# One core's log-sum-exp over 16384 rows: the first 8.4 MB load issued as four loads of growing size

## The chip, the cores and the metric

The kernel runs on one core of one Trainium2 chip. The metric is the time of one execution on the device in microseconds (us), as the median of repeated runs; less is better. A profile of one execution, taken by the hardware profiler, stands beside the times. In it the engines are called ACT (the scalar engine, which does the exponentials), DVE (the vector engine, which does the sums), POOL (the third elementwise engine, which takes part of the sums), PE (the matrix engine, hardly used here) and SP (the engine that issues the transfers). "SPq" is SP's instruction queue.

## The reference

```python
def reference(x):                      # x: float32 [32, 512, 1024]
    max_x = np.max(x, axis=-1, keepdims=True)
    return max_x.squeeze(-1) + np.log(np.sum(np.exp(x - max_x), axis=-1))
```

There are 32 x 512 = 16384 rows of 1024 numbers, 67.1 MB in all, and each gives one number. The inputs are drawn from a standard normal distribution.

## The kernel before, in words

**Rows and partitions.** The 16384 rows are dealt over 128 partitions, 128 rows to each. The first 112 rows of a partition (W) lie next to one another in the input, so that a load of s rows is, for each partition, one stretch of s x 4 KB; neighbouring partitions are 112 x 4 KB = 448 KB apart. The last 16 rows of each partition (B) come from a second region of the input, in which partitions are 64 KB apart.

**Without the maximum.** The kernel takes exp(x) directly, sums it and takes the logarithm. Beside this it keeps a check that no sum has left a range in which that is accurate; only if the check fails does it read everything again and compute the reference's form (L312 to L361). In the profiled execution it does not fail, and this part is a skipped branch at the end.

**Loads and their work.** The table `LOADS` (L23) lists 18 loads by their size in rows of a partition: four of 16 rows (8.4 MB each), then 13.5, 12.5, 9, 7, 6, 4.47 and so on down to 0.53 and 0.47 rows. Beside each size stands what is done with its rows: "R16" is one Exp on ACT over everything (L228) and one summing instruction on DVE (L239); "F" lets POOL first add the two halves of each row (L233), and DVE sums what is left (L171); "T" sums row by row on DVE (L249); the last row comes as "Y" and "Z", in which ACT sums while it takes the Exp (L202).

**The ring.** Data lands in `ring`, 48 rows of each partition. The loads go round it. All of them are issued by SP, in order, by `load` (L134 to L141): ahead of a load that would overwrite rows still in use, SP waits for the DVE or ACT instruction that read them last. The first three loads fill the empty ring and wait for nothing; the fourth waits until DVE has summed the rows of the first.

**What ACT waits for.** Each load has a semaphore of its own, `landed[i]`, which rises by 16 when the whole load has landed. ACT waits for that value before the first Exp on a load (`act.wait(landed[i], 16)` in the loop over the loads, L186 on).

**The opening.** A program begins with barriers in which all engines wait for one another, and only after these come the kernel's instructions: the load of ACT's table (L125), four small DVE memsets (L126 to L129), and SP's loads. The hook `start_early` (L378) moves one instruction: after the program has been built, it takes the first load out of its place and puts it in SP's stream ahead of SP's first DRAIN, which is SP's part in the first barrier. So the first load is issued as the very first instruction, and the second load only after the barriers.

**The end.** While the last loads land, ACT takes the logarithm of the first 112 columns (L268) and SP stores them (L276); the last 16 columns follow (L279, L281, L285), with the check's last steps beside them on DVE and PE (L290 to L308).

Of the kernel before, what the change touches and what calls it, by code (L numbers as in the profile page):

```python
# [15 lines left out]
RING = 48  # L16
B = 16
LATE = 119

# [31 lines left out]
def kernel(  # L53
# [5 lines left out]
    nc = tc.nc  # L59
# [24 lines left out]
    def source(e0, size):  # L84
        assert e0 >= W * d or e0 + size <= W * d
        return x_rest[:, e0 - W * d : e0 - W * d + size] if e0 >= W * d else x_rows[:, e0 : e0 + size]
# [8 lines left out]
    def sbuf(name, cols, dtype=fp32, rows=P):  # L95
        return nc.alloc_sbuf_tensor(name, [rows, cols], dtype).ap()

    ring = sbuf("ring", RING * d)
# [15 lines left out]
    landed = [nc.alloc_semaphore(f"landed{i}") for i in range(len(loads))]  # L114
    act = Counted(nc, nc.scalar, "act")
# [18 lines left out]
    def load(i, here, done_before, size):  # L134
        for a, b, who, at in users:
            if a < here + size and b > here:
                sp.wait(who, at)
        users[:] = [u for u in users if not (u[0] < here + size and u[1] > here)]
        return nc.sync.dma_start(
            out=ring[:, here : here + size], in_=source(done_before, size)  # L140
        ).then_inc(landed[i], 16)  # L141

    def check_early():
        dve.wait(act, summed_by_act)
        dve.wait(dve, dve.n)
        dve.did(nc.vector.tensor_scalar(  # L146
            out=clamped[:, 0:LATE], in0=sumexp[:, 0:LATE],
            scalar1=LOW, scalar2=HIGH, op0=ALU.max, op1=ALU.min,
        ))
        dve.wait(dve, dve.n)  # L150
        dve.did(nc.vector.scalar_tensor_tensor(  # L151
            out=clamped[:, 0:LATE], in0=clamped[:, 0:LATE], scalar=0.0, in1=sumexp[:, 0:LATE],
            op0=ALU.bypass, op1=ALU.not_equal, accum_out=bad[:, 0:1],
# [4 lines left out]
    def add_up(c, who, **kw):  # L158
        pe.wait(*who)
        return pe.did(nc.tensor.matmul(count, lhsT=ones, rhs=sumexp[:, c : c + 1], **kw))  # L160
# [3 lines left out]
    def reduce_folded():  # L164

        nonlocal early_sum
        while folded:
            c0, s0, p0, n0 = folded.pop(0)
            halves = ring[:, p0 : p0 + s0 * d].rearrange("p (c d) -> p c d", d=d)[:, :, 0:H]
            dve.wait(pool, n0)  # L170
            at = dve.did(nc.vector.reduce_sum(  # L171
                out=sumexp[:, c0 : c0 + s0], in_=halves, axis=AX.X
            ))
            users.append((p0, p0 + s0 * d, dve, at))
            if c0 < W:
                early_sum = at
# [3 lines left out]
    here = 0  # L180
    early_sum = 0
    done_before = 0
    summed_by_act = 0
    ln_early = None
    first_load = None
    for i, (size, ops) in enumerate(loads):  # L186
        if here + size > RING * d:
            assert here == p
            p = here = 0
        if any(q < here + size and q + t * d > here for _, t, q, _ in folded):  # L190
            reduce_folded()
        dma = load(i, here, done_before, size)
        first_load = first_load or dma.ins
        end = here + size
        done_before += size
        act.wait(landed[i], 16)
        for k, (how, s) in enumerate(ops):
            rows = ring[:, p : p + s * d].rearrange("p (c d) -> p c d", d=d)
            if how in "YZ":

                assert c == LAST and (how == "Z" or here == p)
                at = act.did(nc.scalar.activation(  # L202
                    out=last_exp[:, here - p : end - p], in_=ring[:, here:end], func=AF.Exp,
                    accum_out=first_sum if how == "Y" else last_sum,
                ))
                if how == "Z":
                    last_piece = ring[:, here:end]
                here = end
                if how == "Y":
                    nc.vector.addr_align(128, offset=0, max_nops=0)  # L210
                    dve.wait(act, at)
                    first_piece = dve.did(nc.vector.tensor_copy(out=sumexp[:, LAST:NC], in_=first_sum))  # L212
                summed_by_act = at
            elif how == "A":
                assert here == p
                v = ring[:, p : p + d]
                at = act.did(nc.scalar.activation(
                    out=v, in_=v, func=AF.Exp, accum_out=sumexp[:, c : c + 1]
                ))
                here += d  # L220
                users.append((p, p + d, act, at))
                summed_by_act = at
                who = (act, at)
            else:

                upto = end if k + 1 == len(ops) and c + s < LAST else p + s * d
                v = ring[:, here:upto]
                at = act.did(nc.scalar.activation(out=v, in_=v, func=AF.Exp))  # L228
                here = upto
            if how == "F":  # L230
                reduce_folded()
                pool.wait(act, at)
                at = pool.did(nc.gpsimd.tensor_tensor(  # L233
                    out=rows[:, :, 0:H], in0=rows[:, :, 0:H], in1=rows[:, :, H:d], op=ALU.add
                ))
                folded.append((c, s, p, at))
            elif how == "R":
                dve.wait(act, at)
                who = (dve, dve.did(nc.vector.reduce_sum(  # L239
                    out=sumexp[:, c : c + s], in_=rows, axis=AX.X  # L240
                )))
                users.append((p, p + s * d, *who))
            elif how == "T":
                if c >= W:
                    reduce_folded()
                dve.wait(act, at)
                for r in range(s):
                    lo = rows[:, r, 0:H]
                    who = (dve, dve.did(nc.vector.scalar_tensor_tensor(  # L249
                        out=lo, in0=lo, scalar=1.0, in1=rows[:, r, H:d],  # L250
                        op0=ALU.mult, op1=ALU.add, accum_out=sumexp[:, c + r : c + r + 1],
                    )))
                    users.append((p + r * d, p + (r + 1) * d, *who))
                    if c + r >= LATE:
                        add_up(c + r, who, start=False, stop=False)
            if how == "A" and c >= LATE:
                add_up(c, who, start=False, stop=False)
            if how in "RT":
                if c < W:
                    early_sum = dve.n  # L260
                reduce_folded()
            c += s
            p += s * d
            if c == LATE:

                act.wait(dve, early_sum)
                act.wait(act, early_act)
                ln_early = act.did(nc.scalar.activation(  # L268
                    out=res[:, 0:W], in_=sumexp[:, 0:W], func=AF.Ln
                ))  # L270
                check_early()
            if c <= W:
                early_act = summed_by_act
        assert here == end
# [7 lines left out]
        out=res[:, LAST:NC], in_=last_sum, func=AF.Ln, bias=sumexp[:, LAST:NC]  # L282
# [7 lines left out]
    dve.did(nc.vector.scalar_tensor_tensor(  # L290
        out=clamped[:, LATE:NC], in0=sumexp[:, LATE:NC], scalar=LOW,
        in1=sumexp[:, LATE:NC], op0=ALU.max, op1=ALU.not_equal, accum_out=bad[:, 1:2],
# [9 lines left out]
        out=over[:, 0:half], in0=last_piece[:, 0:half], scalar=CEILING,  # L302
# [16 lines left out]
    with nc.If(all_fine < 1):  # L319
# [5 lines left out]
        for c0 in range(0, NC, RING):  # L325
# [6 lines left out]
            for c1, c2 in ((c0, edge), (edge, c0 + s)):  # L332
                if c1 == c2:
                    continue
                nc.scalar.dma_start(
                    out=ring[:, (c1 - c0) * d : (c2 - c0) * d],
                    in_=source(c1 * d, (c2 - c1) * d),
# [4 lines left out]
                out=neg, in_=v, op=ALU.max, axis=AX.X, negate=True  # L342
# [3 lines left out]
                out=v, in0=v, in1=neg[:, :, None].to_broadcast([P, s, d])  # L346
# [5 lines left out]
                out=sumexp[:, c0 : c0 + s], in_=v, axis=AX.X  # L352
# [25 lines left out]
    def start_early(program):  # L378

        blocks = program.main_func.blocks  # L380
        here = next(b for b in blocks if any(i.name == first_load.name for i in b.instructions))
        k = next(k for k, i in enumerate(here.instructions) if i.name == first_load.name)
        assert not here.instructions[k].has_wait()
        first = here.instructions.pop(k)
        top = blocks[0].instructions
        k = next(
            k for k, i in enumerate(top)
            if i.engine == mybir.EngineType.SP and isinstance(i, mybir.InstDrain)
        )
        top.insert(k, first)  # L390

    nc.at_finalize(start_early)


# [28 lines left out]
```

## Time and profile before

| what | value |
|---|---|
| time before, median of 3 runs | 161.67 us (161.58 to 161.69) |
| profiled execution: span from its first to its last instruction | 160.4 us |
| what the median has beyond that span | 1.3 us |
| first Exp on ACT starts | 22.00 us after the first instruction |
| second Exp starts | 41.33 us |
| last instruction ends | 160.4 us |

The first instruction of the span is the issue of the first load, and its start is the zero of all times of the trace. No time of its own is listed for the profiled execution apart from its span; the part of a run that lies outside the span is taken from the median, 161.67 - 160.4 = 1.3 us. In the trace an idle stretch of an engine is shown in brackets ahead of the instruction that ended it, with what it had waited for. The lists of transfers count packets in the window in which they start; a load is 128 packets of data, one for each partition, and 16 tiny ones (one for each of the core's 16 DMA engines) that report its end, which gives the page's count: 18 loads and 2 stores of 144 packets are 2880.

### The profile page before, as it was taken

The page shows a single profiled execution, that of the slowest core. Times are in us where ns is not written, and L with a number is a line of the kernel's source. Part 1 is how long each engine was busy: PE and PEld are TensorE (multiplying, and loading weights), DVE is VectorE, ACT ScalarE, POOL GpSimd, SP SyncE. Part 2 cuts the span into 40 slices and gives each one's busy share as a digit, 9 for nine tenths or more (in the row PEclk, how much of TensorE's full clock was granted, in tenths as well). Part 3 has the DMA queues.
Part 4 walks back from the last instruction along what each step waited for, and adds up shares of the span by engine and source line. Part 5 has one row for each costly group of instructions (what it writes and reads, how often), then busy time and mean ns, then how long its engine had stood idle before and what let it go on. Part 6 is the DMA issues. An engine that isn't in the chain of part 4 may idle for free.

```text
span 160.4 us, 219 instructions
## 1 busy us (share of the span) xinstructions
PE 2.2 (1%) x26; PEld 1.1 (1%) x26; DVE 114.3 (71%) x59; ACT 114.5 (71%) x31; POOL 37.3 (23%) x11
## 2 busy tenths in 40 slices
PE   0000000000000000000000000000000000000022
PEld 0000000000000000000000000000000000000011
DVE  0000000009999499994999859959999999999996
ACT  3000059990699708995099949991999989799996
POOL 0000000000000000000000994690004969891000
DMA  7996996996996996996999999999999999999992
GB/s 262 523 523 262 523 523 262 523 507 278 523 490 294 523 490 294 523 490 294 482 441 441 441 425 409 409 409 480 432 395 417 450 416 398 448 411 424 412 413 95
DMA packets 2881, 67.18 MB, mean 419 GB/s; under 512 B 576, under 2 KB 704, under 8 KB 1344
## 3 DMA queue, kind: packets, MB, share of 16 engines
q1 hardware_dynamic: 2880, 67.18, 97.7%
q14 instruction: 1, 0.01, 0.0%
HBM read 67.11 MB, written 0.07 MB: 419 GB/s over the span
## 4 chain that ended last, share of the span: by engine, by line
DMA 52%; ACT 28%; DVE 19%; issue 1%; PE 0%
DMA ring<-in_x_dram 52%; ACT ring L228 27%; DVE sumexp L239 15%; DVE sumexp L171 2%; DVE ring L249 1%; DVE over L301 0%; PE count L306 0%; ACT res L268 0%; DVE clamped L290 0%; DVE fine L308 0%; DVE sumexp L212 0%
## 5 line engine op out<-in xcount | busy, mean ns | idle before, releaser
L228 ACT ACTIVATE ring<-ring 128x16384 f32<-128x16384 f32 (+16 forms) x23 | 111.7, 4908 | 43.0 <-DMA ring<-in_x_dram 43.0
L239 DVE TENSOR_REDUCE sumexp<-ring 128x16 f32<-128x16384 f32 (+4 forms) x9 | 85.6, 9513 | 42.7 <-ACT ring L228 42.7
L233 POOL TENSOR_TENSOR ring<-ring 128x3072 f32<-128x3072 f32 (+3 forms) x7 | 37.1, 5313 | 107.3 <-ACT ring L228 107.3
L171 DVE TENSOR_REDUCE sumexp<-ring 128x6 f32<-128x3072 f32 (+3 forms) x7 | 18.4, 2656 | 0.0
L249 DVE SCALAR_TENSOR_TENSOR ring<-ring 128x512 f32<-128x512 f32 x15 | 9.6, 687 | 0.4 <-ACT ring L228 0.4
L125 ACT ACT_TABLE_LOAD x1 | 1.3, 1283 | 1.4 <-PEq L62 1.4
L156 PE MATMUL count<-far,bad 128*1 128x1 f32 x2 | 0.2, 164 | 153.2 <-DVE clamped L151 153.2
L160 PE MATMUL count<-sumexp,ones 128*1 128x1 f32 x18 | 1.6, 164 | 3.6 <-DVE ring L249 3.6
L249 DVE DVE_READ_ACCUMULATOR ring<-ring 128x1 f32 x15 | 1.2, 82 | 0.0
L202 ACT ACTIVATE last_exp<-ring 128x544 f32<-128x544 f32 (+1 forms) x2 | 1.2, 584 | 0.0
L126 DVE MEMSET ones<- 128x1 f32 x1 | 0.1, 59 | 1.5 <-PEq L62 1.5
L156 PEld LDWEIGHTS count<-far,bad 128*1 128x1 f32 x2 | 0.1, 80 | 153.2 <-DVE clamped L151 153.2
L160 PEld LDWEIGHTS count<-sumexp,ones 128*1 128x1 f32 x18 | 0.8, 80 | 4.5 <-DVE ring L249 4.5
L301 DVE SCALAR_TENSOR_TENSOR over<-ring 128x240 f32<-128x240 f32 x1 | 0.4, 404 | 0.0
L308 DVE TENSOR_SCALAR fine<-count 1x1 int32<-1x1 f32 x1 | 0.1, 147 | 0.3 <-PE count L306 0.3
L151 DVE SCALAR_TENSOR_TENSOR clamped<-clamped,sumexp 128x119 f32<-128x119 f32 x1 | 0.3, 283 | 0.0
L268 ACT ACTIVATE res<-sumexp 128x112 f32<-128x112 f32 x1 | 0.3, 279 | 0.0
L281 ACT ACTIVATE res<-last_sum,sumexp 128x1 f32<-128x1 f32 x1 | 0.3, 261 | 0.0
L202 ACT ACTIVATION_READ_ACCUMULATOR last_exp<-ring 128x1 f32 x2 | 0.3, 126 | 0.0
L146 DVE TENSOR_SCALAR clamped<-sumexp 128x119 f32<-128x119 f32 x1 | 0.2, 221 | 0.0
L279 ACT ACTIVATE res<-sumexp 128x15 f32<-128x15 f32 x1 | 0.2, 209 | 0.0
L290 DVE SCALAR_TENSOR_TENSOR clamped<-sumexp 128x9 f32<-128x9 f32 x1 | 0.2, 169 | 0.0
(17 smaller groups left out, 1.8 us busy)
## 6 DMA issues: line engine op xcount, KB each, us to landing
ring<-in_x_dram SPq DMA_DIRECT2D x1, 6912.0 KB, 23.9
ring<-in_x_dram SPq DMA_DIRECT2D x1, 6400.0 KB, 19.7
ring<-in_x_dram SPq DMA_DIRECT2D x1, 4608.0 KB, 15.9
ring<-in_x_dram SPq DMA_DIRECT2D x1, 3584.0 KB, 24.0
ring<-in_x_dram SPq DMA_DIRECT2D x1, 3072.0 KB, 19.1
ring<-in_x_dram SPq DMA_DIRECT2D x1, 2288.0 KB, 24.1
ring<-in_x_dram SPq DMA_DIRECT2D x1, 1664.0 KB, 20.9
ring<-in_x_dram SPq DMA_DIRECT2D x1, 1264.0 KB, 23.6
```

What stands on the lines that cost most here:

```text
L125: nc.scalar.preload_act_table_set("natural_log_exp_and_others")
L151: dve.did(nc.vector.scalar_tensor_tensor(out=clamped[:, 0:LATE], in0=clamped[:, 0:LATE], scalar=0.0, in1=sumexp[:, 0:LATE], op0=ALU.bypass ...
L156: pe.did(nc.tensor.matmul(count, lhsT=bad[:, 0:1], rhs=far, start=True, stop=False))
L160: return pe.did(nc.tensor.matmul(count, lhsT=ones, rhs=sumexp[:, c : c + 1], **kw))
L171: at = dve.did(nc.vector.reduce_sum(out=sumexp[:, c0 : c0 + s0], in_=halves, axis=AX.X))
L202: at = act.did(nc.scalar.activation(out=last_exp[:, here - p : end - p], in_=ring[:, here:end], func=AF.Exp, accum_out=first_sum if how == ...
L228: at = act.did(nc.scalar.activation(out=v, in_=v, func=AF.Exp))
L233: at = pool.did(nc.gpsimd.tensor_tensor(out=rows[:, :, 0:H], in0=rows[:, :, 0:H], in1=rows[:, :, H:d], op=ALU.add))
L239: who = (dve, dve.did(nc.vector.reduce_sum(out=sumexp[:, c : c + s], in_=rows, axis=AX.X)))
L249: who = (dve, dve.did(nc.vector.scalar_tensor_tensor(out=lo, in0=lo, scalar=1.0, in1=rows[:, r, H:d], op0=ALU.mult, op1=ALU.add, accum_out ...
L268: ln_early = act.did(nc.scalar.activation(out=res[:, 0:W], in_=sumexp[:, 0:W], func=AF.Ln))
L301: dve.did(nc.vector.scalar_tensor_tensor(out=over[:, 0:half], in0=last_piece[:, 0:half], scalar=CEILING, in1=last_piece[:, half : 2 * half ...
```

## The change

The first load (16 rows of each partition) is issued as four: 512, 1024, 2048 and 12800 numbers of each partition, that is half a row, one row, two rows and 12.5 rows. They land next to one another where the one load landed, and come from where it came from. All four raise the same semaphore `landed[0]`, and ACT waits until it has reached 64 in place of 16, so that the first Exp still covers all 16 rows and begins when all four have landed. `start_early` moves all four ahead of SP's first DRAIN, in their order. Nothing else changes; the other 17 loads are one instruction each, as they were.

```diff
+FIRST = [512, 1024, 2048, 12 * 1024 + 512]
...
-        return nc.sync.dma_start(
-            out=ring[:, here : here + size], in_=source(done_before, size)
-        ).then_inc(landed[i], 16)
+        pieces = FIRST if i == 0 else [size]
+        assert sum(pieces) == size
+        made = []
+        for piece in pieces:
+            made.append(nc.sync.dma_start(
+                out=ring[:, here : here + piece], in_=source(done_before, piece)
+            ).then_inc(landed[i], 16))
+            here += piece
+            done_before += piece
+        return made
...
-        dma = load(i, here, done_before, size)
-        first_load = first_load or dma.ins
+        made = load(i, here, done_before, size)
+        first_load = first_load or [dma.ins for dma in made]
...
-        act.wait(landed[i], 16)
+        act.wait(landed[i], 16 * len(made))
...
-        here = next(b for b in blocks if any(i.name == first_load.name for i in b.instructions))
-        k = next(k for k, i in enumerate(here.instructions) if i.name == first_load.name)
-        assert not here.instructions[k].has_wait()
-        first = here.instructions.pop(k)
-        top = blocks[0].instructions
-        k = next(
-            k for k, i in enumerate(top)
-            if i.engine == mybir.EngineType.SP and isinstance(i, mybir.InstDrain)
-        )
-        top.insert(k, first)
+        for load in first_load:
+            here = next(b for b in blocks if any(i.name == load.name for i in b.instructions))
+            k = next(k for k, i in enumerate(here.instructions) if i.name == load.name)
+            assert not here.instructions[k].has_wait()
+            first = here.instructions.pop(k)
+            top = blocks[0].instructions
+            k = next(
+                k for k, i in enumerate(top)
+                if i.engine == mybir.EngineType.SP and isinstance(i, mybir.InstDrain)
+            )
+            top.insert(k, first)
```

## Prediction

> **What bounds the kernel now.** I read the page first: what the DMA engines carry, and the chain that ended last.
>
> ```profile
> span 160.4 us, 219 instructions
> DMA  7996996996996996996999999999999999999992
> DMA packets 2881, 67.18 MB, mean 419 GB/s; under 512 B 576, under 2 KB 704, under 8 KB 1344
> DMA 52%; ACT 28%; DVE 19%; issue 1%; PE 0%
> ```
>
> Half of the chain is transfers, and the mean rate is 419 GB/s. Whether the transfers are also the limit where the chain names ACT and DVE is to be seen in ACT's idle time: the next view is ACT's timeline, each wait in brackets.
>
> ```profile
> 1.45 1.28 ACT L125 ACT_TABLE_LOAD   x1 [1.45 <-PEq L62]
> 22.00 13.86 ACT L228 ACTIVATE ring<-ring 128x16384 f32<-128x16384 f32 x1 [19.27 <-DMA ring<-in_x_dram]
> 41.33 13.86 ACT L228 ACTIVATE ring<-ring 128x16384 f32<-128x16384 f32 x1 [5.46 <-DMA ring<-in_x_dram]
> 60.68 13.86 ACT L228 ACTIVATE ring<-ring 128x16384 f32<-128x16384 f32 x1 [5.49 <-DMA ring<-in_x_dram]
> 80.02 13.95 ACT L228 ACTIVATE ring<-ring 128x9216 f32<-128x9216 f32 x2 [5.49 <-DMA ring<-in_x_dram]
> 96.36 11.82 ACT L228 ACTIVATE ring<-ring 128x6144 f32<-128x6144 f32 x2 [2.39 <-DMA ring<-in_x_dram]
> 111.50 18.89 ACT L228 ACTIVATE ring<-ring 128x6656 f32<-128x6656 f32 x4 [3.32 <-DMA ring<-in_x_dram]
> 130.91 6.27 ACT L228 ACTIVATE ring<-ring 128x4096 f32<-128x4096 f32 x2 [0.53 <-DMA ring<-in_x_dram]
> 138.22 12.34 ACT L228 ACTIVATE ring<-ring 128x2048 f32<-128x2048 f32 x5 [1.04 <-DMA ring<-in_x_dram]
> 150.47 0.28 ACT L268 ACTIVATE res<-sumexp 128x112 f32<-128x112 f32 x1
> 150.66 6.85 ACT L228 ACTIVATE ring<-ring 128x2528 f32<-128x2528 f32 x5
> ```
>
> Up to 138.22 every pause of ACT ends with a landing. From there on it works without a pause, and the rest of the program follows. So the end is the landing that released it at 138.22 plus about 22 us of work. Next, the transfers themselves, between the first landing and the second:
>
> ```profile
> DMA packets 144, 8.39 MB, mean 435 GB/s; under 512 B 16, under 2 KB 16, under 8 KB 16
> q1 hardware_dynamic: 144, 8.39, 100.3%
> ```
>
> This is the window from 22 to 41.3 us: just one load's 144 packets, the 16 DMA engines busy all the time. The landings are 41.33 - 22.00 = 19.33 us apart, as are the next two (19.35, 19.34): 8.39 MB / 19.33 us = 434 GB/s. The stream is at its rate from the first landing on, and SP's waits for ring space don't interrupt it: the load of 4608 KB, the tightest, is issued 15.9 us ahead of its landing and needs 4.72 MB / 434 GB/s = 10.9 us, so that it waits 5 us in the queue.
>
> ```profile
> ring<-in_x_dram SPq DMA_DIRECT2D x1, 4608.0 KB, 15.9
> ```
>
> It follows that **what shifts the stream's start shifts the end by as much**, either way: landings, the ACT and DVE work behind them and the ring's releases move together. An earlier landing at 138.22 finds ACT free, since the landing before it has moved too.
>
> The first load lands at 22.00, though its bytes need 19.33: **2.67 us are start-up**. Only these can shrink. Two windows of the list of transfers, from 1 to 2.5 us and from 5 to 20 us:
>
> ```profile
> DMA packets 16, 1.05 MB, mean 699 GB/s; under 512 B 0, under 2 KB 0, under 8 KB 0
> q1 hardware_dynamic: 16, 1.05, 202.4%
> ```
>
> ```profile
> DMA packets 96, 6.29 MB, mean 419 GB/s; under 512 B 0, under 2 KB 0, under 8 KB 0
> q1 hardware_dynamic: 96, 6.29, 96.8%
> ```
>
> Each engine's first packet (16 packets of 65.5 KB) took on average 2.024 x 1.5 us x 16 / 16 = 3.04 us; later ones took 0.968 x 15 us x 16 / 96 = 2.42 us. So a first packet carries **0.62 us more** than one in the running stream. No packet starts in the first microsecond:
>
> ```profile
> 0.00:1.00 1.00, 0.00 (x0) 0.00 (x0) 0.00 (x0) 0.00 (x0) 0.20 (x4) 1.00 0.00 0
> 1.00:1.50 0.50, 0.00 (x0) 0.00 (x0) 0.00 (x0) 0.05 (x1) 0.00 (x0) 1.00 4.39 1442
> 1.50:2.00 0.50, 0.00 (x0) 0.00 (x0) 0.15 (x4) 0.50 (x1) 0.00 (x0) 1.00 1.35 524
> 2.00:2.50 0.50, 0.00 (x0) 0.00 (x0) 0.00 (x0) 0.50 (x1) 0.00 (x0) 1.00 0.34 131
> ```
>
> By the last column (GB/s), 1442 x 0.5 us = 0.72 MB or 11 first packets start by 1.5 us, 4 by 2.0 and the last by 2.5 us.
>
> **The change part by part.** *SP's issues.* One issue becomes four ahead of the opening barrier. SP's rows:
>
> ```profile
> 0.00 0.39 SPq L139 DMA_DIRECT2D ring<-in_x_dram  x1
> 1.45 0.84 SPq L139 DMA_DIRECT2D ring<-in_x_dram  x2
> 126.64 1.77 SPq L139 DMA_DIRECT2D ring<-in_x_dram  x4
> ```
>
> Four in a row took 1.77 us, 1.38 more than the one. SP comes that much later to its DRAIN, and all engines leave the barriers at about 2.8 in place of 1.45. Behind that stand ACT's table load (1.28 us, done by about 4.1, needed at 22), the DVE memsets (needed after 138) and SP's second and third loads, issued at about 2.8 to 3.7; the DMA engines need the second at about 21.6. The cover is some 18 us; without it the cost would be 1.38 us. I take 0. All six loads then in flight wait for nothing.
>
> *Does the queue run dry between the pieces?* The first piece is 128 x 2 KB = 0.26 MB, 0.60 us at 434 GB/s; the second, 0.52 MB, is issued 1.77 / 4 = 0.44 us behind it. Drained at full rate the first leaves a margin of 0.16 us; the third has 1.81 us of data ahead of it and is issued at 0.89, and so on. If the second's packets reached an engine 0.4 us late against the first's (nothing in the trace excludes that), the gap would be about 0.25 us. I take 0, with bounds 0 and +0.25.
>
> *More and smaller packets.* Per engine the load had 8 data packets and 1 report of its end; it gets 32 and 4, so 27 more. What a packet costs beyond its bytes is read from the window 154 to 156.8 us, where all are small:
>
> ```profile
> DMA packets 457, 1.15 MB, mean 410 GB/s; under 512 B 48, under 2 KB 104, under 8 KB 457
> ```
>
> A packet there has 2516 bytes on average: 16 x 2516 / 410 GB/s = 98.2 ns against 92.8 ns at 434 GB/s, so 5.4 ns. 27 x 5.4 ns = **+0.15 us**, on the path.
>
> *The start-up itself.* The first issue begins at the same moment and takes as long, and the first packets can't start sooner than the 1.0 us above. The trace of before shows no load of 2 KB packets that met idle engines, so this term is bounded. Below: all start-up but the 1.0 us of issue goes, 2.67 - 1.00 = -1.67 us, which would also need the report of the landing to take no time. Nearer: the 0.62 us extra of the first packet goes. Above: each of an engine's 8 first packets pays 0.62 in place of the first alone, +7 x 0.62 = 4.3 us. The nearest row is that of the 16 first packets: the extra is borne once by an engine, whatever 65.5 KB are behind it, and the packet after it, from another partition's stretch 448 KB away, shows none. I take it as a wait for the first bytes, the same for a short packet: 0.
>
> *ACT's wait* for 64 in place of 16 is one wait as before; one summing order, nothing else on DVE, POOL or PE moves.
>
> **Sum:** 0 + 0 + 0.15 + 0 = +0.15 us. The profiled span of 160.4 would be 160.5, and with the 1.3 us around it the median 161.67 + 0.15 = **161.8 us**.
>
> The Trainium skill speaks against the change: "DMA: Bandwidth & Descriptors", section "Anatomy of one DMA", fits a transfer by 2.0 us plus its bytes at 436 GB/s, and its "Rules for kernel authors" want at least 1 MiB per DMA; two pieces are smaller. By that fit, paid one after another, three more DMAs would be an estimated +6 us. That section's fit is for another issue path than SP's.
>
> **The rivals.** *A, the extra of the first packets goes (faster).* Sixteen engines each ask for 65.5 KB at once from idle, and they start up to 1.5 us apart. If this burst makes the 0.62 us, short first packets may get all engines flowing sooner. For it: a later packet takes 2.42 us even where sixteen run together, so the extra belongs to the start. Against it: nothing shows that the burst's size matters rather than its start. Time: 161.67 + 0.15 - 0.62 = 161.2 us; if also the lateness of the last engines shrinks, about 161.0. The Trainium skill's "DMA: Bandwidth & Descriptors", section "Latency and other measured facts", gives 0.2 us for an HBM access and 2 us at high load; a latency that grows with load would favour A, and no run here shows which it is.
>
> *B, cold small packets (slower).* A packet of 65.5 KB covers with its 2.42 us the wait for the next partition's first bytes; one of 2 KB lasts 16 x 2048 / 434 = 0.08 us and covers nothing. If the wait of 0.62 us comes with the first touch of each partition's stretch rather than with the start, the seven further first packets of an engine expose it. For it: 448 KB strides that no small packet of before has walked. Against it: the small packets of the end go from partition to partition too and reach 410 GB/s. It decides from the point where the exposed waits pass 0.2 us together, a third of one. Price: one more wait, +0.6, up to 4.3 if none overlap. I take one: 161.67 + 0.15 + 0.6 = 162.4 us.
>
> *C, each load pays its start anew.* If the pieces ran one after another and each paid the 2.67 us of start-up, +8.0 us: 169.7. Against it: the stream shows no pause where loads meet (100.3% above). This is the fixed cost of the Trainium skill's "DMA: Bandwidth & Descriptors" in the terms of this kernel; by it the pieces would have to wait for one another, and the trace disagrees for queued loads.
>
> *D, the change is not carried out:* the four issues stand at the head of SP's stream in the changed program, in order and ahead of the barrier, so I give it nothing.
>
> **How the numbers follow.** A measurement of this kernel tells about 0.2% from no change, 0.32 us. My forecast (start-up unchanged, +0.1 to +0.3) has 0.40, and it stays within that bound. A beyond the bound has 0.34; a weak A counts with the forecast. B has 0.24, C 0.02. So faster 0.34, same 0.40, slower 0.26. The range reaches from 161.1, a little below A's full price, to 162.5, a little above B with one wait; outside lie A with the engines' lateness gone, B with several waits, and C, together some 0.15 to 0.2.
>
> **What would show it.** The first Exp at 22.15 (A: 21.5 or less; B: 22.7 or more), and every later landing moved by the same amount; the table load at about 2.8 with nothing behind it; four issues in about 1.8 us; the page's packets 432 more, 3313. If the first packets' shares, summed over the first 3 us, show no idle engine once it has begun, the start-up term is right. I am wrong if the first Exp moves by more than 0.3 us, or if the end moves otherwise than the first Exp does: then the claim that the start passes through whole fails.

## The result, and the profile after

The changed kernel takes 162.91 us (median, 162.58 to 163.54) against 161.68 us (161.58 to 161.69) before: a ratio of 1.0080, 95% interval 1.0063 to 1.0097, so about 1.2 us slower. Its runs also lie further apart, by 0.96 us in place of 0.11. The profiled execution took 163.2 us with a span of 161.8, 1.4 more than before.

The page after, in the lines that answer to those of before:

```profile
span 161.8 us, 222 instructions
DMA packets 3313, 67.18 MB, mean 415 GB/s; under 512 B 624, under 2 KB 752, under 8 KB 1648
```

ACT's timeline after, again with each wait in brackets:

```profile
2.87 1.28 ACT L126 ACT_TABLE_LOAD   x1 [2.87 <-PEq L63]
23.44 13.86 ACT L236 ACTIVATE ring<-ring 128x16384 f32<-128x16384 f32 x1 [19.28 <-DMA ring<-in_x_dram]
42.77 13.86 ACT L236 ACTIVATE ring<-ring 128x16384 f32<-128x16384 f32 x1 [5.48 <-DMA ring<-in_x_dram]
...
139.68 12.34 ACT L236 ACTIVATE ring<-ring 128x2048 f32<-128x2048 f32 x5 [1.03 <-DMA ring<-in_x_dram]
...
152.12 6.83 ACT L236 ACTIVATE ring<-ring 128x2528 f32<-128x2528 f32 x5
```

The first Exp starts at 23.44 in place of 22.00. Everything behind it has moved by the same 1.44 to 1.47 us (42.77 against 41.33, 139.68 against 138.22), and each of ACT's waits is as long as it was, within 0.02 us. The whole loss is made before the first landing, and it passes through to the end.

Where in the first load is it made? The list of transfers from 3.5 to 6.1 us, first of the kernel before, then of the changed kernel:

```profile
DMA packets 16, 1.05 MB, mean 403 GB/s; under 512 B 0, under 2 KB 0, under 8 KB 0
q1 hardware_dynamic: 16, 1.05, 93.0%
```

```profile
DMA packets 146, 0.99 MB, mean 381 GB/s; under 512 B 16, under 2 KB 16, under 8 KB 34
q1 hardware_dynamic: 146, 0.99, 103.9%
```

This is the window of the third piece, whose packets are 8 KB. The packets that start in it take 103.9% of the sixteen engines' time together, and yet the rate is only 381 GB/s: packets are open and wait. Most packets of 8 KB take 0.31 us; six that start between 3.79 and 4.76 us take 0.62 to 1.29 us, and some of those behind 5.4 us up to 0.61. The longest stands alone in the list from 4.08 to 4.15 us (114.9% of 16 x 0.07 us is 1.29 us):

```profile
DMA packets 1, 0.01 MB, mean 117 GB/s; under 512 B 0, under 2 KB 0, under 8 KB 0
q1 hardware_dynamic: 1, 0.01, 114.9%
```

In this execution the second piece was slow as well: from 2 to 3.2 us packets of 307 GB/s start, and 394 GB/s in two kernels below that begin with the same two pieces (e4, e12).

And the loss isn't shared evenly. The 16 tiny packets "under 512 B" are the engines' reports that they have ended the first load. Before, all fall between 21.05 and 21.65 us:

```profile
DMA packets 32, 1.05 MB, mean 1748 GB/s; under 512 B 16, under 2 KB 16, under 8 KB 16
```

After, twelve fall between 21.4 and 22.0 us, and the other four between 22.0 and 23.1:

```profile
DMA packets 24, 0.79 MB, mean 1311 GB/s; under 512 B 12, under 2 KB 12, under 8 KB 12
```

```profile
DMA packets 8, 0.26 MB, mean 238 GB/s; under 512 B 4, under 2 KB 4, under 8 KB 4
```

Twelve engines are late by a few tenths, four by 0.6 to 1.4 us. As many were behind at the end of the third piece: twelve engines report that by 6.7 us, and four only between 6.9 and 7.7 us:

```profile
DMA packets 13, 0.25 MB, mean 307 GB/s; under 512 B 4, under 2 KB 4, under 8 KB 4
```

A load has landed only when its last engine has, and an engine that lags has no idle time in which to catch up, so that four engines set the time of the kernel.

### The profile page after: what moved, and what is told of

Read it like the earlier page. It is cut to its first block, busy times and chain, and to the rows that moved or that the text cites. A ratio compares the mean times of both kernels' runs of the same rounds, so it can differ in the third digit from the quotient of the medians.

```text
span 161.8 us, 222 instructions
## 1 busy us (share of the span) xinstructions
PE 2.2 (1%) x26; PEld 1.1 (1%) x26; DVE 114.2 (71%) x59; ACT 114.5 (71%) x31; POOL 37.3 (23%) x11
## 4 chain that ended last, share of the span: by engine, by line
DMA 51%; ACT 27%; DVE 18%; issue 1%; PE 0%
DMA ring<-in_x_dram 51%; ACT ring L236 27%; DVE sumexp L247 15%; DVE sumexp L179 2%; DVE ring L257 1%; DVE over L309 0%; PE count L314 0%; ACT res L276 0%; DVE clamped L298 0%; DVE fine L316 0%; DVE sumexp L220 0%
```

## The experiments

All are the changed kernel with another edit unless said otherwise; ratios are to the kernel before on the same chip. "First Exp" is read in each profile as above: 22.00 us before, 23.44 after.

**Only at the start?** The theory COLD was that small packets are held up only while the engines are starting; its rivals were COUNT (more loads and packets cost this much anywhere) and ISSUE (the issues of the second and third load, at 2.9 to 4.4 us, disturb the small packets).

```diff
-FIRST = [512, 1024, 2048, 12 * 1024 + 512]
+FIRST = [12 * 1024 + 512, 2048, 1024, 512]
```

> The same four pieces, the largest first (12.5, 2, 1 and half a row), so that the small packets come some 15 us later, when the stream is running. Theory COLD (small packets are held up only while the engines are starting): the first Exp at about 22.2 us, time 161.8 us. Theory ISSUE (the issues of the second and third load, at 2.9 to 4.4 us, hold up the small packets that are under way then): also 161.8 us, since no small packet is under way then. Theory COUNT (three more loads and 384 more packets cost about 1.2 us wherever they stand): 162.9 us.

161.82 us, ratio 1.0013 (0.9999 to 1.0027), first Exp at 22.05. COUNT falls.

```diff
-        pieces = FIRST if i == 0 else [size]
+        pieces = FIRST if i == 1 else [size]
```

> The first load whole, as before, and the second load as the four pieces, issued behind the barriers; the engines come to them at about 21 us with the stream running. COLD: only the 0.15 us of more packets, 161.8 us, and no packet of 2, 4 or 8 KB takes much longer than 84, 159 or 309 ns. COUNT: 162.9 us. ISSUE: the third load's issue comes long before the small packets are under way, 161.8 us.

161.93 us, ratio 1.0020 (1.0006 to 1.0034). The same four pieces in the same order, 20 us later, cost 0.3 us, twice what I had put on packets, and a quarter of the loss. And none of its packets of 2, 4 or 8 KB, with the stream running, takes longer than 0.08, 0.16 or 0.31 us. COLD holds so far.

The next two hold the second and third load back by DVE's work on a scratch tile; e5 is the kernel before with that edit.

```diff
+    pause = sbuf("pause", 8)
+    idle_at = dve.did(nc.vector.memset(over, 1.0))
+    dve.wait(dve, idle_at)
+    for q in range(7):
+        idle_at = dve.did(nc.vector.reduce_sum(out=pause[:, q : q + 1], in_=over, axis=AX.X))
...
     def load(i, here, done_before, size):
+        if i == 1:
+            sp.wait(dve, idle_at)
```

> The changed kernel with SP's second and third load held back until about 11 us by seven sums of DVE on a scratch tile; the second is still in the queue some 10 us before it is needed. COLD: the packets of the second and third piece are held up as before, first Exp at about 23.4 us and time about 162.9 us. ISSUE: the hold-ups between 3.8 and 6.5 us go, first Exp at about 22.2 to 22.4 us, time 161.8 to 162.0 us. COUNT: 162.9 us.

> The kernel before with the same hold-back of its second and third load, until about 10 us in place of 1.45 us. ISSUE: a part of the 0.62 us that the first packets take beyond the others goes, first Exp at 21.4 to 21.8 us, time 161.1 to 161.5 us. COLD: the 0.62 us are of the start itself, nothing changes, 161.7 us. COUNT: 161.7 us.

e4: 163.20 us, ratio 1.0102 (1.0069 to 1.0134), first Exp at 22.95. e5: 162.52 us, ratio 1.0056 (1.0042 to 1.0070), first Exp at 22.11:

```profile
22.11 13.86 ACT L235 ACTIVATE ring<-ring 128x16384 f32<-128x16384 f32 x1 [19.38 <-DMA ring<-in_x_dram]
...
156.45 1.03 ACT L235 ACTIVATE ring<-ring 128x992 f32<-128x992 f32 x1 [0.47 <-DMA ring<-in_x_dram]
```

The start of e5 is that of before but for 0.1 us, and e4's is well above 22.2 to 22.4: ISSUE falls. The time of e5 is misleading. It has a wait near the end, at 156.45, that the kernel before doesn't have. In the list of transfers from 154.7 to 155 us a packet of another queue stands among the loads:

```profile
q1 hardware_dynamic: 44, 0.11, 92.2%
q14 instruction: 1, 0.01, 6.9%
```

The kernel before has one such packet (8 KB of instructions, queue q14), at 158.75 us. e5 has one near there too, at 159.4 us, so the one at 154.8 us is a second, and it came with the added instructions. Whether it makes the wait isn't shown: e4 has a second one as well, at 155.5 us, and no wait of ACT's behind it. So the first Exp, not the time, is the reading of these two.

**Which pieces?** Three theories: SIZE or SETTLE (short packets at the start are held up until long ones have brought the sixteen engines into order), STEP or GROWTH (each step from short to longer packets costs), TOUCH (the first short packet in each partition's stretch pays). Each edit is another `FIRST`, in numbers of 4 bytes:

```diff
+FIRST = [512, 15 * 1024 + 512]                  # e7
+FIRST = [4096, 4096, 4096, 4096]                # e8
+FIRST = [4096, 512, 1024, 2048, 8 * 1024 + 512] # e9
+FIRST = [2048, 1024, 512, 12 * 1024 + 512]      # e10
```

> Two pieces, half a row and 15.5 rows. What is known by now: small packets are held up only at the start. Theory SIZE (a small packet at the start exposes waits that a long one covers, each piece of small packets adds its share): only the first of three small pieces is left, a third of the loss or less, first Exp at 22.1 to 22.5 us, time 161.8 to 162.1 us. Theory STEP (the hold-ups come where an engine passes from short to longer packets and asks for far more at once, while others are behind): one step, and the largest, first Exp at 22.6 us or later, time 162.3 us or more. Theory TOUCH (the first touch of each partition's stretch by a short packet is what is paid): all of it is paid in the first piece, 162.5 us or more.

> Four pieces of four rows each, packets of 16 KB, four issues ahead of the barrier as in the changed kernel. SIZE: a packet of 0.61 us covers most of a wait, first Exp at 22.05 to 22.5 us, time 161.8 to 162.2 us. STEP: no step to longer packets but the last to the second load's, 161.8 us. TOUCH: 161.8 us. That four issues ahead of the barrier are what costs: 162.9 us.

> Five pieces: four rows first (16 KB packets, 4.8 us of data), then half a row, one row, two rows and 8.5 rows, so that the three small pieces come at about 7 to 12 us. SIZE, if the start is over once the first long packets are through: first Exp at 22.2 us, time 161.8 to 161.9 us. STEP: the same steps as in the changed kernel, 162.5 us or more. TOUCH: 161.8 us.

> The same four sizes, with the three small ones in the order two rows, one row, half a row, and then 12.5 rows. The same number of small packets at the start, but they grow only once, at the end. SIZE: as the changed kernel, first Exp at 23.0 us or later, time 162.6 to 163.2 us. STEP: hold-ups only at the passage to 12.5 rows, at about 5.5 us; first Exp at 22.2 to 22.8 us, time 161.9 to 162.5 us. TOUCH: the first packets are 8 KB in place of 2 KB and pay a part, 162.2 to 162.9 us.

e7 161.55 us, ratio 0.9990 (0.9981 to 1.0000); e8 161.77, 1.0001 (0.9991 to 1.0010); e9 161.80, 1.0008 (0.9998 to 1.0017); e10 161.59, 0.9990 (0.9980 to 0.9999). None has the loss. e8 and e9 show that four or five issues ahead of the barrier cost nothing. e7 begins with the same 2 KB packets and takes the largest step of all, so STEP and TOUCH fall; e10 has all the short packets of the changed kernel at the start, so SIZE falls as I had put it. And in e7 and e10 the first Exp starts sooner than in the kernel before, at 21.83 and 21.72.

```diff
+FIRST = [2048, 14 * 1024]            # e11
+FIRST = [512, 1024, 14 * 1024 + 512] # e12
+FIRST = [512, 2048, 13 * 1024 + 512] # e13
+FIRST = [512, 512, 512, 14 * 1024 + 512] # e14
```

> Two pieces, two rows and 14 rows: the kernel with the fewest pieces that starts on 8 KB packets, which the shrinking order started on. Theory GROWTH (the engines lose time each time they pass, soon after the start, from short packets to longer ones) and theory SETTLE (they lose time until packets are long enough for the sixteen to fall into a steady order) both: first Exp at 21.6 to 21.8 us, time 161.4 to 161.6 us. If the shrinking order owed its time to the two small pieces behind the first: first Exp at 22.0 us, 161.7 us.

> Half a row, one row, 14.5 rows: the changed kernel without the piece of two rows. GROWTH: two steps up in place of three, first Exp at 22.2 to 22.7 us, time 161.9 to 162.4 us. SETTLE: short packets for 1.8 us and then long ones, on which the engines settle: 21.9 to 22.3 us, 161.6 to 162.0 us. If the piece of two rows alone carries the loss: as with half a row and 15.5 rows, 21.83 us and 161.55 us.

> Half a row, two rows, 13.5 rows: the changed kernel without the piece of one row. GROWTH: two steps up, first Exp at 22.2 to 22.7 us, time 161.9 to 162.4 us. SETTLE: after a start on 2 KB packets, 8 KB are long enough, as they were from rest: 21.8 to 22.1 us, 161.5 to 161.8 us. If 8 KB packets after a start on short ones are what is held up: 22.7 to 23.5 us, 162.4 us or more.

> Three pieces of half a row and then 14.5 rows: as many bytes in short packets as with half a row, one row and 14.5 rows, in more packets, but without growth among them. GROWTH: as with half a row and 15.5 rows, first Exp at 21.8 to 22.0 us, time 161.5 to 161.7 us. SETTLE: 24 short packets for each engine ahead of the first long one, so worse than half a row, one row and 14.5 rows: 22.2 to 22.8 us, 161.9 to 162.5 us.

e11 161.40 us, ratio 0.9987 (0.9978 to 0.9995), faster than both kernels; e12 163.54, 1.0117 (1.0099 to 1.0134); e13 161.58, 0.9995 (0.9985 to 1.0005); e14 164.13, 1.0157 (1.0140 to 1.0175). Their first Exps, in this order:

```profile
21.56 13.86 ACT L236 ACTIVATE ring<-ring 128x16384 f32<-128x16384 f32 x1 [18.36 <-DMA ring<-in_x_dram]
```

```profile
23.27 13.86 ACT L236 ACTIVATE ring<-ring 128x16384 f32<-128x16384 f32 x1 [19.59 <-DMA ring<-in_x_dram]
```

```profile
21.63 13.86 ACT L236 ACTIVATE ring<-ring 128x16384 f32<-128x16384 f32 x1 [17.95 <-DMA ring<-in_x_dram]
```

```profile
24.01 13.86 ACT L236 ACTIVATE ring<-ring 128x16384 f32<-128x16384 f32 x1 [19.85 <-DMA ring<-in_x_dram]
```

e14 has no growth among its short pieces and loses most: GROWTH falls too. So does SETTLE, which allowed 162.0 us for e12 and 162.5 us for e14. What divides these runs is how much data lies in the queue ahead of the *third* load (its bytes at 434 GB/s):

| first pieces, in rows | data ahead of the third load | ratio to before |
|---|---|---|
| 0.5, 0.5, 0.5, 14.5 (e14) | 1.2 us | 1.0157 |
| 0.5, 1, 14.5 (e12) | 1.8 us | 1.0117 |
| 0.5, 1, 2, 12.5 (the change; with the next loads held back, e4) | 1.8 us | 1.0080 (1.0102) |
| 0.5, 1.5, 14 (e19, below) | 2.4 us | 0.9991 |
| 0.5, 2, 13.5 (e13) | 3.0 us | 0.9995 |
| 2, 1, 0.5, 12.5 (e10) | 3.6 us | 0.9990 |
| 4, 0.5, 1, 2, 8.5 (e9) | 5.4 us | 1.0008 |
| 4, 4, 4, 4 (e8) | 9.7 us | 1.0001 |

In e7 and e11 the third load is the next one of 16 rows, 19 us behind the start. e12 shows what happens to an engine. SP issues its third load within the first 1.33 us:

```profile
0.00 1.33 SPq L144 DMA_DIRECT2D ring<-in_x_dram  x3
```

From 3.15 to 3.95 us all sixteen engines report the end of the second load (the 16 under 512 B):

```profile
DMA packets 49, 0.91 MB, mean 1137 GB/s; under 512 B 16, under 2 KB 16, under 8 KB 35
```

Yet two engines begin their first long packet only later, at 3.96 and 4.7 us. The list from 4 to 5 us has the second of them alone; in its 40 slices it stands in the thirtieth:

```profile
GB/s 0 0 0 0 0 0 0 0 0 0 0 0 0 0 0 0 0 0 0 0 0 0 0 0 0 0 0 0 0 2376 0 0 0 0 0 0 0 0 0 0
DMA packets 1, 0.06 MB, mean 59 GB/s; under 512 B 0, under 2 KB 0, under 8 KB 0
q1 hardware_dynamic: 1, 0.06, 17.8%
```

That engine had nothing to do for 0.8 us or more, with the third load issued 3.4 us before, and its packet then takes 2.85 us (17.8% of 16 x 1 us). The packet of 3.96 us takes 3.15 us, those of the fourteen other engines 2.2 to 2.3. With seven more packets of 2.19 us each, the two engines should end the load at about 4.72 + 2.85 + 15.33 = 22.9 and 3.96 + 3.15 + 15.33 = 22.4 us. So they do: fourteen engines report the end between 21 and 21.6 us, two between 22 and 23 us (at 22.44 and 22.90), and the first Exp starts at 23.27:

```profile
DMA packets 28, 0.92 MB, mean 1529 GB/s; under 512 B 14, under 2 KB 14, under 8 KB 14
```

```profile
DMA packets 4, 0.13 MB, mean 131 GB/s; under 512 B 2, under 2 KB 2, under 8 KB 2
```

So in e12 these two engines make the loss: they start the third load late, and their first packet of it is long besides. In e14, whose third piece is short too, more engines are in that state. From 3.39 to 3.72 us 0.33 MB begin, which is five long packets of 59 KB beside short ones:

```profile
DMA packets 29, 0.33 MB, mean 987 GB/s; under 512 B 10, under 2 KB 10, under 8 KB 24
```

From 3.72 to 4.36 us, while those five run on (2.2 to 2.6 us each), the other eleven engines begin only eight short packets among them:

```profile
DMA packets 8, 0.02 MB, mean 26 GB/s; under 512 B 0, under 2 KB 0, under 8 KB 8
q1 hardware_dynamic: 8, 0.02, 28.4%
```

One other thing sets the table's runs with the loss apart: in each of them a load begins 1.5 rows into the partition's stretch, in none of the others. e14 speaks against it as the cause, since the short packets that come late there belong to its third load, which begins at one row; it was not tried by itself.

**Late loads or short packets?** Theory LATE: at the start, the third and later loads reach some engines only some microseconds after their issue, and engines run dry if little is queued ahead. Theory SHORT: sixteen or more short packets of an engine are themselves held up. e15 and e16 put many 2 KB packets into *one* load (the first halves of 3 or 7 rows), the long rest second, the other halves third; e17 is e11 with its first piece as two loads of 64 partitions.

```diff
+cut = lambda v, h: v[:, 0 : ROWS * d].rearrange("p (c d) -> p c d", d=d)[:, :, h * H : h * H + H]
+parts = [(cut(to, 0), cut(src, 0)), (to[:, ROWS * d : size], src[:, ROWS * d : size]), (cut(to, 1), cut(src, 1))]
...
+            for q in (slice(0, P // 2), slice(P // 2, P)) if i == 0 and k == 0 else (slice(0, P),):
+                made.append(nc.sync.dma_start(out=to[q], in_=src[q]).then_inc(landed[i], 16))
```

> The first load as three: one load of the first halves of rows 0 to 2 (24 packets of 2 KB for each engine, as many as in three loads of half a row, but in one load), then rows 3 to 15, then the second halves of rows 0 to 2, which come when the stream is running. Theory SHORT (16 or more short packets of an engine at the start are themselves what is held up): as three loads of half a row, first Exp at 23.3 to 24.2 us, time 163.2 to 164.2 us. Theory LATE (a load issued at the start reaches some engines only some us after its issue, the third and later ones up to 4 us, and the engines run out of work when the loads ahead of it are short): the second load is needed at about 2.8 us and was there by 2.5 us in the runs with half a row first; no loss but the packets' own, first Exp at 21.8 to 22.2 us, time 161.5 to 161.9 us.

> The same with the halves of rows 0 to 6: 56 packets of 2 KB for each engine in one load, 4.7 us of data, then 9 rows, then the other halves. SHORT: more short packets than in any kernel so far, first Exp at 23.5 us or later, time 163.2 us or more. LATE: the second load is needed at about 5.7 us, long after it has reached all engines; first Exp at 21.9 to 22.3 us, time 161.6 to 162.0 us.

> Two rows and 14 rows, which took 161.4 us, with the two rows issued as two loads of 64 partitions each: the same 8 packets of 8 KB for each engine ahead of the long ones, but in two loads of 1.2 us of data, so that the 14 rows are the third load, needed at about 3.4 us. SHORT: no packet is shorter than 8 KB, no loss, first Exp at 21.5 to 21.9 us, time 161.3 to 161.7 us. LATE: the third load comes late to some engines, as after half a row and one row: first Exp at 22.5 us or later, time 162.3 us or more.

e15 161.93 us, ratio 1.0013 (1.0003 to 1.0022), first Exp at 22.08, where e14 with as many short packets in three loads had 24.01. So short packets by themselves don't carry the loss. e16 162.85 us, 1.0065 (1.0049 to 1.0082), between the two forecasts: I had left out the price of its 114 extra packets. Its list of transfers from 18 to 21.5 us, with 2 KB packets alone and the stream running:

```profile
DMA packets 660, 1.35 MB, mean 386 GB/s; under 512 B 0, under 2 KB 0, under 8 KB 660
```

16 x 2048 / 386 = 84.9 ns in place of 75.5 at 434 GB/s, 9.4 ns a packet; 114 of them are 1.07 us, about the difference to the 161.75 of before, 1.10.

e17 163.77 us, 1.0125 (1.0109 to 1.0142), but it didn't test LATE. From 2.7 to 5.4 us its loads of 64 partitions ran at 240 GB/s with all engines occupied. By an estimate from that rate the 1.05 MB of the two rows take 4.37 us in place of 2.42, which is 1.95 us of the 2.48 by which its first Exp (24.04) is behind that of e11:

```profile
DMA packets 95, 0.65 MB, mean 240 GB/s; under 512 B 16, under 2 KB 16, under 8 KB 16
q1 hardware_dynamic: 95, 0.65, 109.9%
```

The Trainium skill ("DMA: Bandwidth & Descriptors", "Rules for kernel authors") advises against splitting a load by partition halves, because both halves use the same engines. The run agrees: all sixteen engines report the end of one half in this window. At the start of this program the price was nearly half the rate.

**Which queue, and how much is enough?**

```diff
-            made.append(nc.sync.dma_start(
+            made.append((nc.scalar if i == 0 and k >= 2 else nc.sync).dma_start(   # e18
...
+FIRST = [512, 1536, 14 * 1024]   # e19
```

> The changed kernel with its third and fourth piece issued by ACT, ahead of ACT's part in the opening barrier, in place of SP: both are issued in the first microsecond on another queue. LATE, if the lateness of the third load belongs to its place in SP's queue: it reaches the engines as the first of its own queue; first Exp at 22.4 us or earlier, time 162.0 us or less. LATE, if the issue of several loads is worked off one after another for all queues: first Exp at 22.8 us or later, time 162.4 us or more. SHORT: as the changed kernel, 162.6 to 163.5 us.

> Half a row, one and a half rows, 14 rows: the third load is needed at about 3.8 us, between half a row, one row, 14.5 rows (3.2 us, 163.5 us) and half a row, two rows, 13.5 rows (4.6 us, 161.6 us). LATE: a loss between the two, first Exp at 22.0 to 22.9 us, time 161.8 to 162.8 us. SHORT (packets of 2 KB and 6 KB, 16 to an engine, as with one row): the same loss as there, 163 us or more, or as with two rows, 161.6 us, but none in between.

e18 163.78 us, 1.0120 (1.0094 to 1.0145), but for a new reason: ACT's queue (q10) and SP's (q1) shared the engines. From 5 to 17 us 114 packets of SP's second piece, 4 KB each, stand beside 124 of ACT's, most of them long, so that the second piece landed only 20.1 us after its issue:

```profile
ring<-in_x_dram SPq DMA_DIRECT2D x1, 512.0 KB, 20.1
```

The second load of 16 rows then went beside the rest of ACT's, and the first Exp started only at 27.40. As to what it was made for, from 2.6 to 5 us the engines were hardly ever dry:

```profile
DMA packets 159, 1.01 MB, mean 421 GB/s; under 512 B 15, under 2 KB 15, under 8 KB 43
...
q10 hardware_dynamic: 116, 0.95, 98.2%
q1 hardware_dynamic: 43, 0.06, 6.7%
```

That fits a lateness which belongs to a load's place in its own queue, but an engine that always has two queues to draw on needs each of them less, so it isn't shown.

e19 161.56 us, 0.9991 (0.9981 to 1.0000), first Exp at 21.61. I had expected a loss between those of e12 and e13; there is none. So it isn't a loss that fades evenly: 1.8 us of data ahead of the third load was too little here, 2.4 us enough.

## Why the prediction was wrong

- **What passes through.** Right: landings, waits and end all moved with the first Exp (1.44 us there, 1.4 in the span).
- **SP's issues and the barrier.** Right: four issues took 1.81 us (0.00 to 1.81), the table load moved to 2.87, and nothing was late behind it; e8 and e9 had as many issues and no loss.
- **"Does the queue run dry between the pieces?"** This step failed. I compared the data of a piece with SP's pace of *issuing*, 0.44 us a load, took the second piece as the tight one and the third as safe with 1.81 us of data ahead, and bounded the term at +0.25 us. The runs showed the opposite: a second load with only 0.6 us ahead of it costs nothing (e7, e13), while a third with 1.8 us or less ahead is not there in time on some engines (e12's two engines without work until 3.96 and 4.7 us, which make its whole loss). The term is about 1.3 us: the changed kernel against e13, which lacks only the piece of one row, 1.0080 against 0.9995. In the changed kernel itself little of this shows as idle engines; six packets of its third piece are open for 0.62 to 1.29 us in place of 0.31 (none of the same size in e13 for more than 0.55), and four engines end that piece late. e12's late engines had both, no work and then a long first packet. That both are one cause is inferred from this and from the table, not shown.
- **More and smaller packets**, +0.15 us: right in kind, too small. In the running stream it was 0.2 to 0.3 us (e1, e6), with 9.4 ns for a packet of 2 KB in place of 5.4 ns; I had averaged over a window whose rate is read to a few GB/s.
- **The start-up itself**, taken as unchanged: wrong by -0.2 to -0.4 us. With 2 KB or 8 KB packets first and no loss behind them, the first Exp comes at 21.83 (e7) to 21.56 (e11), and e11's time is 0.3 us below before. Rival A was right in this effect; that the size of the first burst makes it isn't shown. In the changed kernel the gain is covered by the loss.
- **Rival B**, at 162.4 us, came nearest to the measured 162.9, but by luck: its mechanism isn't there, since 24 short first packets in one load cost no such waits (e15).
- **Rival C** and the estimate from the Trainium skill's fit, 2.0 us for each load, are far off: one to four more loads at the start cost nothing (e7, e8, e9) or, with little queued ahead of the third, 1.2 to 2.4 us in all (the change, e12, e14).

Open: why the third load comes late to some engines, why the limit is so sharp, and why the changed kernel, with as much data ahead of its third load as e12, loses less.

## What to carry to other kernels

At the start of a program a load that has been issued may not yet be at every engine (in e12 one engine began on it 3.4 us after the issue): give the first two loads together some microseconds of data before a third is needed (here 1.8 us was too little and 2.4 enough), or split only in two. A short first load can shorten the start, by 0.2 to 0.4 us of the first landing here; the ladder of short ones that was tried gave back more than that. When a stream that is never idle is late, look at the spread of the engines' reports: four slow engines of sixteen set every landing behind them.

## What the hardware showed beyond that

- At the start of the program, loads over 64 of the 128 partitions ran at 240 GB/s, with all sixteen engines occupied, against 434 GB/s for loads over 128 in the running stream (e17).
- With eight more DVE instructions, one more instruction packet of 8 KB (queue q14) stood in the stream of loads, in e5 at 154.8 us and in e4 at 155.5 us. In e5 ACT then waited 0.47 us for data, in e4 it did not.
- Loads on SP's and ACT's queue shared the engines, and an early issue gave no precedence: SP's piece of 512 KB, issued in the first microsecond beside two loads of ACT's, landed 20.1 us after its issue, and the first Exp started 5.4 us later than before (27.40 against 22.00, e18). The Trainium skill's "DMA: Bandwidth & Descriptors", "Issuing engines are not separate DMA queues", says that they interleave on the same engines; the trace agrees.
